# Where h and the tiles after it begin in on-chip memory, and when the first projection weights are made ready

## The chip, the cores and the metric

The kernel runs on one core of a Trainium2 chip. The metric is the device time of the whole program in microseconds (us), the median of several executions. The core has five engines that run side by side and wait for each other through semaphores: TensorE (PE, matrix products, with its own weight load, PEld), VectorE (DVE), ScalarE (ACT), GpSimd (POOL) and SyncE (SP, which issues nearly all of the DMAs here). Each engine takes its instructions in a fixed order that is written when the program is built.

A matrix product has a *stationary* operand, which is loaded into the array first, and a *moving* operand, which streams past it. Both are read from the on-chip memory (128 partitions; an address here is a byte offset within a partition).

## The reference

One layer of a hybrid decoder over 1024 tokens of width 1024, all in float32:

```
h = RMSNorm(x)
z = h @ W_in                       # 1024 -> 8224 columns
A = rwkv7(z_a)                     # time mixing, 8 heads x 64, delta-rule state
B = rglru(z_bx) * gelu(z_by)       # conv of width 4, then a linear recurrence
C = dilated_attention(z_q,z_k,z_v) # three head groups, joined by softmax sums
x = x + W_out(sum_b sigmoid(z_g[b]) * P_b(y_b))     # P_b: proj_a, proj_b, proj_c
x = x + W_down(relu(W_up RMSNorm(x))^2)             # 1024 -> 4096 -> 1024
```

## The kernel before, in words

Every large product is made of three products in a faster 32-bit format: an operand is split into a high and a low part (`A.copy(hi, raw)` on ACT, then `raw - hi` on DVE or POOL), and `mm3` issues high x high, high x low and low x high into the same PSUM bank (lines 234 to 236). `load_w` (lines 220 to 228) fetches a weight block into `wraw` (two buffers), and splits it into `whi` and `wlo` (three buffers each).

The stages, with the names under which the profile shows their matmuls:

- to 52 us: RMSNorm and the transposes (`nt_m`), which write h, transposed and split, into eight tiles `hh`, `hl` (high and low; two halves of the width, two of the tokens; 8 KB a partition each).
- 52 to 174 us: branch B (`g_bx`, `g_by`); from 130 us the projections of branch A (`g_xwa`, `g_xg`, `g_k`, `g_r`, `g_v`), then its recurrence (`ac`, `rg`, `z` and others), with the attention's projections (`g_z`, `v`) as filler between its steps, to 804 us. In `v` the h tile is stationary and the weights (256 columns) move; in the other projections the weights are stationary and 512 tokens of h move.
- 804 to 1151 us: the attention, with the merge gates (`gate_z`, matmuls `zg`) as filler. `gate_z` makes its first two of twelve pairs of column blocks plainly, and the other ten by seven block products in place of eight, for which it builds the combinations `zT1` to `zT4` of h.
- 1151 to 1272 us: `gates`, the three branch projections (`pj`) in four rounds over the output columns, in each the branches B, A, C; the branch outputs `y` come from DRAM through `wraw` (`load_y`: DMA, cast on ACT, subtraction on DVE or POOL by turns) and are split into tiles that take the places of the combinations (`y1T2`, `y1T1`, `y0T3`) or lie in a pool of their own (`yp`).
- 1272 to 1365 us: `wo`, the product with `w_out`, whose stationary operand is the merged sum (`mh`, `ml`, in the places of h).
- 1365 to 1686 us: the up product (`ux`, `uy`, `uz`), also by seven block products, with moving operands `B11`, `B21`, `T2`, `T1`, `T3`, `B22`, `T4`.
- 1686 to 2006 us: the down product (`dx`, `dy`, `dz`), in which `du`, the split activations, are stationary and the weights move.

On-chip memory is given out as two stacks. The left stack grows upwards: `cp` (constants: `cg`, `par`, `der`, `sst` and a tile of padding), `wp` (the weight buffers), then the pools of the stage. The right stack grows downwards from the end: pool `hT` with the eight h tiles, and below it `hS` for the combinations. When h is no longer used, other tiles take its eight places: `zT4`, then `mh` and `ml`, and in the tail whatever has a tag `r0` to `r7`; the tail's tags `l0` to `l12` lie in the left stack. The tail's operands are

```
operand("B11", "l8", "l9")   operand("B21", "l10", "l11")
T2: ("r5", "r6")   T1: ("l1", "r4")   T3: ("l6", "l7")   B22: ("l12", "l0")   T4: ("r7", "l2")
uring = ("r5", "r6", "l1", "r4")      # the places of du, in turn
```

where the first tag is the high part and the second the low part.

In the program before, the end of the right stack is at byte 229,344 = 224 x 1024 - 32. All tiles of `hT` and `hS` have sizes that are multiples of 1 KB, so each of them begins 992 bytes into a KB. `wp` begins at 19,456 = 19 x 1024, and the matmul operands in `wp`, in `yp` and under the `l` tags all begin at multiples of 1 KB.

The order around the second part of the change: in the last of the twelve pairs of `gate_z`, after its second block product, `late[0]()` is called, which loads the four tiles of `yb`. The weights of the first projection block (`p10`, from `proj_b`) are loaded after that, as the first thing in `gates`. All of these loads, and those of `ya`, `yc` and the next weights, go through the two `wraw` buffers in the order of the program.

Of the kernel before, what the change touches and what calls it, by code (L numbers as in the profile page):

```python
# [10 lines left out]
F32 = mybir.dt.float32  # L11
# [7 lines left out]
P = 128  # L19
# [105 lines left out]
def hybrid_block(ctx, tc, io, out, dbg=None):  # L125
# [4 lines left out]
    cp = ctx.enter_context(tc.tile_pool(name="cp", bufs=1))  # L130
    wp = ctx.enter_context(tc.tile_pool(name="wp", bufs=1))
    dr = ctx.enter_context(tc.tile_pool(name="dr", bufs=1, space=DRAM))
    pg = ctx.enter_context(tc.tile_pool(name="pg", bufs=2, space=PSUM))
# [6 lines left out]
    yb_d = dr.tile([LW, T], F32, name="yb_d")  # L140
    yc_d = dr.tile([2 * P, T], F32, name="yc_d")
# [7 lines left out]
    io = dict(io)  # L149
    io["st_d"] = dr.tile([3, 2, 32, P], F32, name="st_d")  # L150
    th_d = dr.tile([3, KT, P, T], F32, name="th_d")

    hpool = tc.tile_pool(name="hT", bufs=1, side="right")
    hp = hpool.__enter__()

# [18 lines left out]

    par = cp.tile([P, N_PAR], F32, name="par")
    der = cp.tile([P, 64], F32, name="der")

    sst = cp.tile([P, 3, 2, 2, 2, 8], F32, name="sst")

    cp.tile([P, 120], F32, name="pad")  # L180
    V.memset(der[:, 63:64], 1.0)
    A.activation(der[:, 63:64], der[:, 63:64], AF.Sqrt)
    rows = lambda ap: ap.rearrange("o (r c) -> (o r) c", c=P)
# [55 lines left out]
    def load_cols(w2d, c0, n, nm, E=G):  # L239
        return load_w(w2d[:, c0 : c0 + n].rearrange("(k p) c -> p k c", p=P), [P, KT, n], nm, E)  # L240
# [42 lines left out]
    with tc.issue_after(done.ins):  # L283
        w0 = {(0, x): load_cols(w_in, c, P, f"w0{x}", V) for x, c in enumerate((C_BX, C_BY))}
# [39 lines left out]
    gt = gt_p.__enter__()  # L324
    h2_p = tc.tile_pool(name="hS", bufs=1, side="right")
    h2 = h2_p.__enter__()
    late = []
# [3 lines left out]
    yp = yp_p.__enter__()  # L331
    ys = {}

    def load_y(src, b, ks, place):

        for k in ks:
            r = wp.tile([P, T], F32, tag="wraw", name=f"yr{b}{k}", bufs=2)
            S.dma_start(r, src[k * P : (k + 1) * P, :])
            h, l = (place(k, x) for x in "hl")
            A.copy(h, r)  # L340
            (G if k % 2 else V).tensor_tensor(l, r, h, ALU.subtract)
            ys[(b, k)] = h, l
# [3 lines left out]
    def in_block(nm, b):  # L346

        def place(k, x):
            if k % 2 == 0:
                blocks[(b, k // 2, x)] = h2.tile([P, 2, T], F32R, tag=f"{nm[k // 2]}{x}", name=f"y{b}{nm[k // 2]}{x}")  # L350
            return blocks[(b, k // 2, x)][:, k % 2, :]
        return place

    in_yp = lambda b: lambda k, x: yp.tile([P, T], F32R, name=f"y{b}{k}{x}")
    late.append(lambda: load_y(yb_d, 1, range(4), in_block(("T2", "T1"), 1)))
    for _ in fill:
        pass

# [4 lines left out]
    mhi, mlo = ([[mt[(x, hf, k // 4)][:, k % 4, :] for hf in range(2)] for k in range(KT)] for x in range(2))  # L363
    def load_ya():
        load_y(ya_d, 0, range(2), in_block(("T3",), 0))
        load_y(ya_d, 0, range(2, 4), in_yp(0))

    last = gates(tc, io, psum, pg, gt, yp, wp, th_d, ys, mhi, mlo, load_w, mm3, {0: load_ya, 2: lambda: load_y(yc_d, 2, range(2), in_yp(2))})
    yp_p.__exit__(None, None, None)
    gt_p.__exit__(None, None, None)  # L370
    h2_p.__exit__(None, None, None)
# [969 lines left out]
            yield  # L1341


def gates(tc, io, psum, pg, gt, tp, wp, th_d, ys, mhi, mlo, load_w, mm3, loads):

    nc = tc.nc
    V, A, G, S = nc.vector, nc.scalar, nc.gpsimd, nc.sync
    names = {1: "proj_b", 2: "proj_c", 0: "proj_a"}
    turn = 0
    for p in range(KT // 2):  # L1350
        sums = {}
        for b in (1, 0, 2):
            kn = 2 if b == 2 else 4
            w = io[names[b]][0][:, 2 * p * P : (2 * p + 2) * P]
            wh, wl = load_w(w.rearrange("(k p) c -> p k c", p=P), [P, kn, 256], f"p{b}{p}")
            if p == 0 and b in loads:
                loads[b]()
            tiles = [(m, hf) for m in (2 * p, 2 * p + 1) for hf in range(2)]
            bk = [pg.tile([P, 512], F32, tag="g", name=f"pj{b}{p}{i}") if i < 2 else psum("w", 2, f"pj{b}{p}{i}") for i in range(4)] if turn % 2 else [
                psum("s", 2, f"pj{b}{p}{i}") if i < 2 else psum(f"ac{i - 2}", 1, f"pj{b}{p}{i}") for i in range(4)]  # L1360
            turn += 1
            for (m, hf), ps in zip(tiles, bk):
                sl, ms = slice(hf * H, hf * H + H), slice(m % 2 * P, (m % 2 + 1) * P)
                th = (tp.tile([P, H], F32, tag="tb", name=f"tb{b}{m}{hf}", bufs=8) if b == 1 else
                      gt.tile([P, H], F32, tag="th", name=f"tg{b}{m}{hf}", bufs=5))
                last = S.dma_start(th, th_d[b, m, :, sl])
                mm3(ps, [(wh[:, k, ms], wl[:, k, ms], ys[(b, k)][0][:, sl], ys[(b, k)][1][:, sl]) for k in range(kn)])
                V.scalar_tensor_tensor(th, th, 1.0, ps, ALU.add, ALU.mult)
                if b == 1:
                    sums[(m, hf)] = th  # L1370
                    continue
                s = sums[(m, hf)]
                V.tensor_tensor(s, s, th, ALU.add)
                if b == 2:
                    A.activation(mhi[m][hf], s, AF.Copy, scale=0.5)
                    V.scalar_tensor_tensor(mlo[m][hf], s, 0.5, mhi[m][hf], ALU.mult, ALU.subtract)
    return last
# [378 lines left out]
```

## Time and profile before

| | us |
|---|---|
| median of three runs (lowest, highest) | 1999.5 (1998.18, 2002.98) |
| the profiled execution | 2007.88 |
| its span, first to last instruction | 2006.1 |
| PE busy | 1937.7 |
| DVE busy | 1240.2 |
| POOL, ACT busy | 773.7, 762.8 |
| granted TensorE clock, mean share | 0.985 |

The profile is of one execution. A row of a group of instructions reads: line, engine, operation, output <- inputs by the program's names, shape, count, then busy us, mean ns of one instruction, idle time of the engine just before them and what ended it. A row in order of time reads: start us, duration us, engine, line and so on. Matmuls are pipelined: the drawn duration of one reaches into the next ones, so the pace of a run of them is read from the distance of their starts. In the windows' rows, each engine's busy time is followed by the number of instructions.

### The profile page before, as it was taken

The numbers are of one execution on the slowest core, as the hardware profiler recorded it, in microseconds if no ns is written. First come the engines' busy times: TensorE is split into PE (matmuls) and PEld (weight loads), VectorE is DVE, ScalarE is ACT, GpSimd is POOL, SyncE is SP. The second block draws the span as 40 slices with busy tenths as digits, with TensorE's granted clock in tenths as the row PEclk, the third lists the DMA queues.
The fourth block names the chain that finished last, engine by engine and source line by source line (L and its number), as shares of the span: only waits on it lengthen the run. The fifth ranks groups of instructions, "written<-read, shape, count | busy, mean of one in ns | idle before, by whom it ended". The sixth has DMA issues, their size and how long they took to land. (4 is left out here: it accounts for less than half of the span.)

```text
span 2006.1 us, 29767 instructions
## 1 busy us (share of the span) xinstructions
PE 1937.7 (97%) x11634; PEld 1515.7 (76%) x11634; DVE 1240.2 (62%) x1992; ACT 762.8 (38%) x1275; POOL 773.7 (39%) x631
## 2 busy tenths in 40 slices
PE   8999999999999999999999899999999999999999
PEld 6776777786677778777767668887788888788887
DVE  5555446556566554775454456347876677987875
ACT  5675323233323322445454321245233233333332
POOL 1343533443343340622532442344334344544542
PEclk9999999999999998999999999999999999999999
DMA  4122312221221221434442664542444439535231
GB/s 145 53 70 70 102 37 61 63 62 51 51 59 50 65 54 42 129 105 149 143 134 90 190 225 158 184 158 105 158 168 147 147 144 366 194 125 188 85 126 63
DMA packets 191618, 236.53 MB, mean 118 GB/s; under 512 B 38536, under 2 KB 133413, under 8 KB 191478
## 3 DMA queue, kind: packets, MB, share of 16 engines
q1 hardware_dynamic: 191302, 234.62, 35.6%
q8 instruction: 91, 1.49, 0.3%
q14 instruction: 49, 0.40, 0.1%
q0 software_dynamic: 160, 0.02, 0.0%
q10 hardware_dynamic: 16, 0.00, 0.0%
HBM read 168.14 MB, written 68.82 MB: 118 GB/s over the span
## 5 line engine op out<-in xcount | busy, mean ns | idle before, releaser
L1476 POOL TENSOR_TENSOR wl_d<-dr,wh_d 128x1024 fp32r<-128x1024 f32 x40 | 102.4, 2560 | 131.7 <-ACT wh_d L1475 131.7
L1285 POOL TENSOR_TENSOR wz<-wr_z,wz 128x512 fp32r<-128x512 f32 x60 | 82.5, 1375 | 169.3 <-ACT wz L1284 145.5
L1476 DVE TENSOR_TENSOR du<-dq,du 128x1024 fp32r<-128x1024 f32 x56 | 123.7, 2208 | 26.9 <-ACT du L1475 26.9
L234 PE MATMUL dx<-wh_d,du 128*128 128x512 f32 x256 | 101.6, 397 | 2.6 <-DVE acc L1656 2.6
L235 PE MATMUL dx<-wl_d,du 128*128 128x512 f32 x256 | 101.2, 395 | 0.0
L236 PE MATMUL dx<-wh_d,du 128*128 128x512 f32 x256 | 101.1, 395 | 0.0
L1475 ACT CAST wh_d<-dr 128x1024 fp32r<-128x1024 f32 x40 | 42.0, 1050 | 145.3 <-PE dx L236 75.5
L771 DVE TENSOR_SCALAR s<-ac,wc 64x64 f32<-64x64 f32 x128 | 36.0, 281 | 71.8 <-PE ac L767 69.4
L235 PE MATMUL g_z<-hl,wh_z 128*128 128x512 f32 x192 | 77.9, 406 | 0.0
L236 PE MATMUL g_z<-hh,wl_z 128*128 128x512 f32 x192 | 77.7, 405 | 0.0
L234 PE MATMUL g_z<-hh,wh_z 128*128 128x512 f32 x192 | 77.2, 402 | 0.4 <-DVE zsq L426 0.4
L1476 POOL TENSOR_TENSOR wl_a<-ur,wh_a 128x1024 fp32r<-128x1024 f32 x15 | 47.3, 3156 | 72.9 <-ACT wh_a L1475 72.9
L1476 POOL TENSOR_TENSOR wl_s<-ur,wh_s 128x1024 fp32r<-128x1024 f32 x16 | 41.7, 2608 | 82.1 <-ACT wh_s L1475 82.1
L227 POOL TENSOR_TENSOR wl_wo<-wr_wo,wh_wo 128x1024 fp32r<-128x1024 f32 x16 | 39.2, 2452 | 64.6 <-ACT wh_wo L226 64.5
L1475 ACT CAST du<-dq 128x1024 fp32r<-128x1024 f32 x56 | 58.6, 1046 | 3.3 <-DMA dq<-u_d 3.3
L1656 DVE TENSOR_TENSOR acc<-dx,acc 128x512 f32<-128x512 f32 x64 | 42.0, 679 | 28.3 <-PE dx L236 28.3
L234 PEld LDWEIGHTS dx<-wh_d,du 128*128 128x128 f32 x256 | 48.4, 189 | 14.3 <-DVE acc L1656 3.0
L234 PE MATMUL v<-wh_wv,hh 128*128 128x256 f32 x192 | 56.3, 293 | 1.3 <-DVE st L777 1.3
L235 PEld LDWEIGHTS dx<-wl_d,du 128*128 128x128 f32 x256 | 48.4, 189 | 11.4
L236 PEld LDWEIGHTS dx<-wh_d,du 128*128 128x128 f32 x256 | 48.3, 189 | 11.5
L1022 DVE SCALAR_TENSOR_TENSOR lg<-l,sst,bias 128x128 f32<-128x128 f32 (+1 forms) x96 | 34.3, 403 | 36.2 <-PE pt L1042 27.5
L235 PE MATMUL v<-wl_wv,hh 128*128 128x256 f32 x192 | 55.6, 290 | 0.0
(757 smaller groups left out, 6213.6 us busy)
## 6 DMA issues: line engine op xcount, KB each, us to landing
dq<-u_d SPq DMA_DIRECT2D x56, 512.0 KB
wr_z<-in_w_in_dram SPq DMA_DIRECT2D x32, 512.0 KB
ur<-in_mlp_up_dram SPq DMA_DIRECT2D x16, 1024.0 KB
dr<-in_mlp_down_dram SPq DMA_DIRECT2D x16, 1024.0 KB
th_d<-th SPq DMA_DIRECT2D x48, 256.0 KB
tg<-th_d SPq DMA_DIRECT2D x32, 256.0 KB
wr_wo<-in_w_out_dram SPq DMA_DIRECT2D x16, 512.0 KB
qk_d<-zo SPq DMA_DIRECT2D x24, 256.0 KB
```

What stands on the lines that cost most here:

```text
L227: E.tensor_tensor(lo, raw, hi, ALU.subtract)
L234: PE.matmul(ps, lh, rh, start=first and i == 0, stop=False, skip_group_check=skip)
L235: PE.matmul(ps, lh, rl, start=False, stop=False, skip_group_check=skip)
L236: end = PE.matmul(ps, ll, rh, start=False, stop=last and i == n - 1, skip_group_check=skip)
L771: V.tensor_scalar(ns[half[h], :], pb[h][half[h], 128 * j + 64 * c : 128 * j + 64 * c + 64], wc[half[h], 2 * i + c : 2 * i + c + 1], None, ...
L1022: V.scalar_tensor_tensor(lg[:, q, lo:256], pls[h][:, 256 * q + lo : 256 * q + 256], rqk[:, 8 * h + s : 8 * h + s + 1], bias[:, h, lo:256], ...
L1285: (V if i == 2 else G).tensor_tensor(l, src, h, ALU.subtract)
L1475: A.copy(hi, src)
L1476: split.last = E.tensor_tensor(lo, src, hi, ALU.subtract)
L1656: V.tensor_tensor(acc[row][:, half[col]], ps, acc[row][:, half[col]], ALU.add)
```

## The change

It has two parts. The tile `sst` (768 bytes a partition), until now in `cp`, and a padding tile of 224 bytes are put into a new pool at the end of the right stack, ahead of `hT`; the padding in `cp` shrinks from 480 to 224 bytes. So the right stack begins 992 bytes lower and `hT`, `hS` and all that takes their places begin at multiples of 1 KB; `cp` is 1024 bytes shorter, and the left stack begins a whole KB lower. And the weights `p10` are loaded and split in `late[0]()`, ahead of the four `yb` loads, and handed to `gates` as `w0`.

```diff
+    cr = ctx.enter_context(tc.tile_pool(name="cr", bufs=1, side="right"))
+
+    sst = cr.tile([P, 3, 2, 2, 2, 8], F32, name="sst")
+    cr.tile([P, 56], F32, name="padr")
     hpool = tc.tile_pool(name="hT", bufs=1, side="right")
     hp = hpool.__enter__()
...
     der = cp.tile([P, 64], F32, name="der")
-
-    sst = cp.tile([P, 3, 2, 2, 2, 8], F32, name="sst")
-
-    cp.tile([P, 120], F32, name="pad")
+    cp.tile([P, 56], F32, name="pad")
...
-    late.append(lambda: load_y(yb_d, 1, range(4), in_block(("T2", "T1"), 1)))
+    def load_first():
+        late.append(load_w(io["proj_b"][0][:, 0:256].rearrange("(k p) c -> p k c", p=P), [P, 4, 256], "p10"))
+        load_y(yb_d, 1, range(4), in_block(("T2", "T1"), 1))
+
+    late.append(load_first)
...
-    last = gates(tc, io, psum, pg, gt, yp, wp, th_d, ys, mhi, mlo, load_w, mm3, {0: load_ya, 2: lambda: load_y(yc_d, 2, range(2), in_yp(2))})
+    last = gates(tc, io, psum, pg, gt, yp, wp, th_d, ys, mhi, mlo, load_w, mm3, late[1], {0: load_ya, 2: lambda: load_y(yc_d, 2, range(2), in_yp(2))})
...
-            wh, wl = load_w(w.rearrange("(k p) c -> p k c", p=P), [P, kn, 256], f"p{b}{p}")
+            wh, wl = w0 if (b, p) == (1, 0) else load_w(w.rearrange("(k p) c -> p k c", p=P), [P, kn, 256], f"p{b}{p}")
```

More of the change, by code (lines that the diff above doesn't have):

```diff
@@ L1341, in gate_z, with gates @@
             yield
-def gates(tc, io, psum, pg, gt, tp, wp, th_d, ys, mhi, mlo, load_w, mm3, loads):
+def gates(tc, io, psum, pg, gt, tp, wp, th_d, ys, mhi, mlo, load_w, mm3, w0, loads):
     nc = tc.nc
```

## The prediction

> **What bounds the kernel now.** I read the page's head first, then the windows by stage, then the waits of TensorE, then the matmul groups of one stage, and at last the order of time at two places.
>
> ```profile
> span 2006.1 us, 29767 instructions
> PE 1937.7 (97%) x11634; PEld 1515.7 (76%) x11634; DVE 1240.2 (62%) x1992; ACT 762.8 (38%) x1275; POOL 773.7 (39%) x631
> ```
>
> TensorE is busy in 97% of the span, and the next engine, DVE, in 62%. The span less PE's busy time leaves 2006.1 - 1937.7 = 68.4 us in which PE stands still. Where these lie, the windows say (the first engine column is PE, then PEld, DVE, ACT, POOL, the granted clock, DMA):
>
> ```profile
> 52.00:131.00 79.00, 74.62 (x312) 58.93 (x311) 42.40 (x63) 51.01 (x56) 30.11 (x15) 0.98 0.21 58
> 822.00:1104.00 282.00, 277.13 (x1412) 201.36 (x1413) 162.33 (x348) 143.43 (x398) 112.99 (x89) 0.99 0.38 119
> 1104.00:1152.00 48.00, 39.10 (x163) 30.50 (x160) 23.11 (x34) 17.75 (x29) 22.32 (x14) 0.96 0.60 187
> 1425.00:1686.00 261.00, 259.99 (x1131) 211.81 (x1130) 177.32 (x139) 82.00 (x106) 102.71 (x34) 1.00 0.49 181
> 1686.00:2006.00 320.00, 313.68 (x1347) 253.12 (x1345) 253.09 (x201) 106.60 (x107) 140.84 (x54) 0.99 0.40 144
> ```
>
> Every long stage is PE's; only the hand-over around 1104 to 1152 us is not (39.1 of 48). The page draws matmuls overlapped, so a busy PE may still be paced by something. So the question is what paces a matmul that waits for nothing.
>
> **What alignment is worth: the up stage shows it in one kernel.** By the layout of the program before, the right-hand stack ends 32 bytes below a multiple of 1 KB, so every tile there (`r0` to `r7` in the tail, all of h, its combinations, y in their places) begins 992 bytes into a KB; all matmul operands of the left stack (`wp`, the `l` tags) begin at multiples of 1 KB. In the up product the weights are stationary in `wp` and the moving operand is T2 (both halves right), T1 (h left, l right), T4 (h right, l left), T3, B22, B11, B21 (left). Same shape, same weights' place, same 260 us, with PE waiting 1 us in it:
>
> ```profile
> L234 PE MATMUL ux<-T2h,wh_s 128*128 128x512 f32 x56 | 22.3, 398 | 1.0 <-ACT c L1493 1.0
> L235 PE MATMUL ux<-T2l,wh_s 128*128 128x512 f32 x56 | 22.2, 396 | 0.0
> L236 PE MATMUL ux<-T2h,wl_s 128*128 128x512 f32 x56 | 22.1, 396 | 0.0
> ...
> L235 PE MATMUL ux<-T3l,wh_s 128*128 128x512 f32 x56 | 21.9, 391 | 0.0
> ...
> L234 PE MATMUL uz<-B22h,wh_s 128*128 128x512 f32 x56 | 21.8, 389 | 0.0
> L235 PE MATMUL uz<-B22l,wh_s 128*128 128x512 f32 x56 | 21.8, 389 | 0.0
> ...
> L236 PE MATMUL ux<-T4h,wl_a 128*128 128x512 f32 x55 | 21.8, 395 | 0.0
> ...
> L235 PE MATMUL ux<-B11l,wh_a 128*128 128x512 f32 x48 | 18.8, 391 | 0.0
> ```
>
> Off the KB a matmul takes 395 to 398 ns, on it 389 to 391: a gap of 4 to 9 ns. Since drawn durations overlap, the spacing counts:
>
> ```profile
> 1429.74 0.40 PE L234 MATMUL ux<-T2h,wh_s 128*128 128x512 f32 x1
> ...
> 1432.54 0.39 PE L234 MATMUL uz<-T1h,wh_s 128*128 128x512 f32 x1
> ...
> 1443.65 0.39 PE L234 MATMUL uz<-B22h,wh_s 128*128 128x512 f32 x1
> ...
> 1448.86 0.39 PE L236 MATMUL uz<-B22h,wl_s 128*128 128x512 f32 x1
> ```
>
> Twelve starts of T2 in 1432.54 - 1429.74 = 2.80 us are 233.3 ns each; 23 steps of B22 in 5.21 us are 226.5. So 6.8 ns, or 2.9%, per matmul of 512 columns. A stationary operand off the KB with the moving one on it shows the slow figure too (`wo`, where `mh` is stationary on the right):
>
> ```profile
> L235 PE MATMUL wo<-wl_wo,mh 128*128 128x512 f32 x128 | 50.7, 396 | 0.0
> L236 PE MATMUL wo<-wh_wo,ml 128*128 128x512 f32 x128 | 50.5, 395 | 0.0
> ```
>
> **The change, part by part.**
> *Layout.* `sst` (768 bytes a partition) and 224 bytes of padding now lie at the right end, 992 bytes in all, so the right stack begins on a KB; `cp` loses 768 + 256 = 1024 bytes, so the left stack moves by one whole KB and keeps its places. No instruction is added; `sst` is read as before. What moves to the aligned pace, counted from the loops and these rows (PE count by window; first the matmuls that read `hh`, then `hl`):
>
> ```profile
> 0.00:52.00 52.00, 24.75 (x70) 0.93 0.44 140
> 52.00:174.00 122.00, 92.86 (x284) 0.97 0.21 61
> 174.00:804.00 630.00, 333.41 (x1152) 0.98 0.22 59
> 804.00:1104.00 300.00, 112.89 (x328) 0.99 0.40 125
> 1104.00:1152.00 48.00, 13.33 (x40) 0.96 0.60 187
> ```
> ```profile
> 52.00:174.00 122.00, 57.54 (x143) 0.97 0.21 61
> 174.00:804.00 630.00, 210.87 (x576) 0.98 0.22 59
> ```
>
> `hl` has half of `hh`'s count, in each stage: 1.5 x 1874 = 2811, by the loops 2808 (a window's edge counts twice). Of them 576 are the 256-column products of `v` (24 tiles x 8 x 3), where h is stationary; 2232 have 512 columns. Further by the loops: combinations in `gate_z` 4 x 10 pairs x 12 = 480; y in their places 6 x 48 = 288; `wo` 384; up: T2 192, `T1l` 64, `T4h` 128; down: 1344, whose stationary `du` goes round `r5, r6, l1, r4`, so three in four, 1008. Sum: 2232 + 480 + 288 + 384 + 384 + 1008 = 4776 matmuls of 512.
>
> Price: the groups bound it at 4 and 9 ns, the two runs in order of time give 6.8; I take 6.0, because the `T3l` and `B11l` groups on the KB sit at 391 and not at 389. That is 4776 x 6.0 = 28.7 us. For the 576 of 256 columns no row has an aligned partner (they stand at 287 to 293 ns); bounds 0 (if the loss goes with the length read at a stretch) and 6 (one fixed loss a matmul); I take 3, 1.7 us. Sum 30.4 us if PE were alone.
>
> How much reaches the end? Where others pace, a shorter matmul only lengthens PE's wait. To 174 us (532 matmuls of h; norm, DVE and ACT chains), in 1104 to 1182 us (60 + 96 of `gate_z`, 72 of y) and in the opening of up (48) I count half: 808 x 6.0 / 2 = 2.4 us lost. In the stretches where a recurrence or softmax is interleaved (174 to 1104 us: 1152 + 492 + 384 = 2028 matmuls and the 576), PE is nearly always busy (277 of 282 us in the softmax's stretch) and the others mostly wait for it, as the scan's step shows: DVE waited 69 us for PE there, PE 2.2 for DVE.
>
> ```profile
> L771 DVE TENSOR_SCALAR s<-ac,wc 64x64 f32<-64x64 f32 x128 | 36.0, 281 | 71.8 <-PE ac L767 69.4
> ```
> ```profile
> PE ac L764 <- DVE s L771: 2.2, 4, 0.8
> ```
>
> There I take off 15% of 13.9 us, 2.1 us. The other 1940 (rest of y, `wo`, up, down: 11.6 us) pass in full; DVE covers down with 253 of 320 us. Kept: 30.4 - 2.4 - 2.1 = 25.9 us. What the places do to DVE, ACT, POOL and the DMAs I cost at nothing: none of them is the bound of a long stage, so a few per cent of theirs, up or down, vanish in their slack (in down DVE has 320 - 253 = 67 us).
>
> *The first projection weights in the last pair.* `load_w` of `proj_b` (one 512 KB DMA on SP, one 1.05 us cast on ACT, one 2.4 us subtraction on POOL) moves from behind the four `yb` loads to ahead of them, past SP, ACT and POOL queues; nothing is added.
>
> ```profile
> 1131.12 0.40 PE L236 MATMUL zg<-zT2h,wz 128*128 128x512 f32 x1
> 1133.12 1.26 POOL L1285 TENSOR_TENSOR wz<-wr_z,wz 128x512 fp32r<-128x512 f32 x1
> 1135.92 0.79 PE L234 MATMUL zg<-zT1h,wz 128*128 128x512 f32 x1 [4.40 <-DVE th L1328]
> 1136.60 3.52 POOL L1121 TENSOR_TENSOR yc<-yc,yt 128x512 f32<-128x512 f32 x2 [2.22 <-DVE yc L1116]
> 1145.52 0.41 SPq L223 DMA_DIRECT2D wr_p<-in_proj_b_dram  x1
> 1150.69 1.04 ACT L226 CAST wh_p<-wr_p 128x1024 fp32r<-128x1024 f32 x1 [1.26 <-DMA wr_p<-in_proj_b_dram]
> 1151.79 0.50 PE L234 MATMUL pj<-y1T2h,wh_p 128*128 128x512 f32 x1 [3.05 <-ACT wh_p L226]
> 1152.59 0.63 PE L235 MATMUL pj<-y1T2l,wh_p 128*128 128x512 f32 x1
> ...
> 1156.00 0.39 PE L236 MATMUL pj<-y1T2h,wl_p 128*128 128x512 f32 x1
> 1175.77 1.56 SPq L338 DMA_DIRECT2D yr<-yc_d  x2
> ```
>
> PE waits 3.05 us for these weights and then runs eight matmuls in 1156.00 - 1152.59 = 3.41 us, 0.43 us each (drawn 0.63 long) and not 0.23: 1.6 us more. 4.6 us is the upper bound. (The clock gate of the Trainium skill, "TensorE: Matmul & The Clock Gate", "What's actually happening", halves the clock after an idle window of about 3.4 us; the rows after both waits agree.) But the raw weights and y go through two `wraw` buffers, each load waiting for the POOL or DVE subtraction two loads back, down to the `yc` loads at 1175.77, and putting the weights first leaves as many loads in this chain. If POOL makes their low half only behind `yc` (1136.60 + 3.52 = 1140.1, done at 1142.5), the second `yb` load is late next, and some 2 us may be lost: lower bound -2. PE's first 36 matmuls cover the late fourth `yb` tile; then y of A is waited for instead. I take +2.
>
> Sum: 25.9 + 2 = 27.9 us. The profiled execution is 2007.9 us (span 2006.1 and 1.8 around it) and would be 1980.0; it stands 8.4 above the median of the runs, 1999.5, from which the same 27.9 leaves 1971.6.
>
> **The rivals.**
> *A: the layout changes nothing.* Then the slow pace belongs to the right stack's high addresses, not to the 32 bytes, and only the weights count: 1999.5 - 2 = 1997.5. For it: no right-hand tile is seen aligned. Against it: `B22h` lies above 150 KB in the partition, between the places where `zT1` was slow, and is fast. The Trainium skill speaks for it twice: by "TensorE: Matmul & The Clock Gate" ("Wait — 56ns, not 53.3ns?") a warm matmul starts every N / 2.4 GHz + 2.5 ns, 215.8 ns for 512, wherever its operands lie; by "SBUF — State Buffer" ("Specifications (TRN2)") lines have 16 bytes, and 992 is a multiple of that. The trace agrees with neither: 226.5 and 233.3 ns stand side by side.
> *B: the pace falls, but the gain stops at others' waits.* PE's 68.4 us of standing then grow: half of 30.4 lost, none from the weights, 1999.5 - 15.2 = 1984.3. For it: 2028 of the matmuls are filler between chains of others. Against: the scan's waits above.
> *C: slower.* With weights and h beginning at the same offset in the KB, weight load and moving read would meet at the same place and each matmul would lose the 6.8 ns once more: 4776 x 6.8 = 32.5 us, 2032. It decides as soon as pairs on the KB are slower than mixed ones. Against: `B22` with `wp` is such a pair, and the fastest.
>
> **How the numbers follow.** Forecast 0.73, B 0.13, A 0.09, C 0.05. The range: 4 ns in place of 6 gives 1999.5 - 17 - 2 = 1980; with 6.8 for all, 3.5 for the narrow ones, nothing lost and 4.6 for the weights, 32.5 + 2.0 + 4.6 = 39 and 1960.5. The likeliest case alone is 1961 to 1981; with B 1961 to 1988, leaving out A and C (0.14). About 0.3% (6 us) is what a measurement here can tell: forecast and B are faster by more; A splits into 0.07 same, 0.01 faster, 0.01 slower; C is slower. Faster 0.87, same 0.07, slower 0.06.
>
> **What the changed profile would show.** Right: `T2`, `T4` and `wo` groups at 389 to 391 ns like `B22`; `g_z` (402 to 406 now) lower by about 6; the down stage some 6 us shorter than 320, up 2 to 3; no wait of `pj` for `wh_p` at its start, but one for a y tile within 20 us. Wrong: these groups at 395 and more (A), or all at 400 (C); or the groups fall and the waits of PE grow by 10 us and more (B).

## The result, and the profile after

| | before | changed |
|---|---|---|
| median (lowest, highest), four runs each, us | 2001.24 (1998.18, 2005.46) | 1982.83 (1979.91, 1986.43) |
| ratio, with its 95% interval | | 0.9907 (0.988 to 0.9935) |
| profiled execution, us | 2007.88 | 1979.91 |
| its span, us | 2006.1 | 1978.1 |

The changed kernel is faster by 0.93%, some 18.6 us (13 to 24 by the interval). The forecast was 1971.6, with a range from 1961 to 1988. The sign holds. The time lies inside the range only because the range took in rival *B*; the likeliest case alone was 1961 to 1981, and 1982.83 is outside it. A third of the forecast gain of 27.9 us is missing. (The forecast was taken from a median of 1999.5 over three runs; with the fourth the kernel before stands at 2001.24, which is 1.7 of the 11.2 us between forecast and result.) In the ratios below one execution is left out, of the kernel with the right stack 64 bytes off: it took 3733.11 us, its nine others 1995.61 to 2002.65.

The two profiled spans differ by 28.0 us, which looks like the forecast exactly, but it isn't: the profiled execution of before lies above all four of its runs in the table, that of the changed kernel is the quickest of its four (granted clock 0.985 and 0.988; the other three took 1980.97 at 0.987, 1984.69 and 1986.43 at 0.985). A difference of two spans holds that spread, so the reading below goes by the pace of the matmuls (the time from the start of one to the start of the next) and not by the spans.

The head of the page after:

```profile
span 1978.1 us, 29765 instructions
PE 1906.3 (96%) x11634; PEld 1512.1 (76%) x11634; DVE 1237.5 (63%) x1992; ACT 763.5 (39%) x1275; POOL 774.5 (39%) x631
```

As many matmuls as before, 31.4 us less of TensorE's drawn time, and 1978.1 - 1906.3 = 71.8 us of standing still, 3.4 more than before. The windows of the softmax's stretch, the up stage and the down stage (320 us long before, 310 now):

```profile
822.00:1104.00 282.00, 275.74 (x1436) 202.84 (x1435) 162.46 (x356) 146.84 (x406) 117.39 (x91) 1.00 0.38 120
1425.00:1686.00 261.00, 261.00 (x1154) 216.10 (x1153) 183.77 (x142) 83.30 (x106) 106.05 (x35) 1.00 0.51 194
1668.00:1978.00 310.00, 305.84 (x1349) 252.58 (x1347) 248.06 (x199) 106.75 (x107) 138.97 (x54) 1.00 0.40 147
```

In the same 282 us lie 1436 matmuls for 1412, in the same 261 us 1154 for 1131, and the down stage needs 310 us for what took 320. (The windows are fixed in time and the stages begin earlier now: the last 17 us of the second window belong to the down product already.) The groups of matmuls in the up stage, where the moving operands T2, T1 and T4 stood beside T3, B22 and B11 at another figure:

```profile
L238 PE MATMUL ux<-T4h,wl_a 128*128 128x512 f32 x58 | 22.6, 389 | 0.0
L236 PE MATMUL ux<-T2h,wh_s 128*128 128x512 f32 x56 | 21.9, 391 | 0.6 <-ACT c L1499 0.6
...
L237 PE MATMUL ux<-T3l,wh_s 128*128 128x512 f32 x56 | 21.8, 389 | 0.0
L236 PE MATMUL uz<-B22h,wh_s 128*128 128x512 f32 x56 | 21.8, 389 | 0.0
```

All are alike now. In the groups of the whole program, the drawn means of `g_z` and `v` (filler between the steps of other chains) have changed little, that of `wo` by 6 ns:

```profile
L237 PE MATMUL g_z<-hl,wh_z 128*128 128x512 f32 x192 | 77.4, 403 | 0.0
...
L237 PE MATMUL v<-wl_wv,hh 128*128 128x256 f32 x192 | 55.6, 290 | 0.0
...
L237 PE MATMUL wo<-wl_wo,mh 128*128 128x512 f32 x128 | 49.9, 390 | 0.0
```

In the trace of before, the same `g_z` and `v` groups:

```profile
L235 PE MATMUL g_z<-hl,wh_z 128*128 128x512 f32 x192 | 77.9, 406 | 0.0
...
L235 PE MATMUL v<-wl_wv,hh 128*128 128x256 f32 x192 | 55.6, 290 | 0.0
```

So three things had to be explained: whether the layout is all of the gain, what it is in the layout that counts, and why the filler gains so little.

**The measure used below.** Drawn durations overlap, so for every split-format matmul (the ones that `mm3` issues, and the 48 of `zss` in the attention's projections) the distance from its start to the next start was taken, cut off at 245 ns (128 ns for 256 columns) where something else came between, and added up by stage. The rest of the span is waits, other matmuls and cut-off ends. This sum is called the pace sum below. In us:

| stage | before | layout only (below) | difference |
|---|---|---|---|
| start to the first `g_k` | 134.6 | 132.8 | 1.8 |
| from there to the last `v` | 350.0 | 347.1 | 2.9 |
| to the last `zg` | 242.5 | 238.5 | 4.0 |
| `pj` | 111.7 | 109.7 | 2.0 |
| `wo` | 89.6 | 87.2 | 2.4 |
| up | 309.2 | 305.4 | 3.8 |
| down | 311.4 | 304.5 | 6.9 |
| all | 1549.0 | 1525.2 | 23.8 |

The pace sum is a steady figure: it is 1525.0 in the changed kernel and 1524.9 in a second profile of it, and 1549.1 in the kernel with the weights alone, while the rest of the span moves between 451 and 461 us from one execution to the next.

### The profile page after: what moved, and what is told of

The parts are those of the page before. It is cut to its first block, busy times and chain, and to the rows that moved or that the text cites. A ratio compares the mean times of both kernels' runs of the same rounds, so it can differ in the third digit from the quotient of the medians.

```text
span 1978.1 us, 29765 instructions
## 1 busy us (share of the span) xinstructions
PE 1906.3 (96%) x11634; PEld 1512.1 (76%) x11634; DVE 1237.5 (63%) x1992; ACT 763.5 (39%) x1275; POOL 774.5 (39%) x631
## 4 chain that ended last, share of the span: by engine, by line
PE 77%; DVE 8%; DMA 6%; ACT 3%; issue 3%; POOL 3%; SPq 1%; DVEq 0%; ACTq 0%; POOLq 0%
PE dx L236 3%; PE dx L237 3%; PE dx L238 3%; PE zg L236 3%; PE ux L236 3%; PE ux L237 3%; PE ux L238 3%; PE zg L237 3%; PE zg L238 3%; PE g_z L237 2%; PE g_z L236 2%; PE g_z L238 2%; PE wo L238 1%; PE wo L236 1%; PE dz L237 1%
## 5 line engine op out<-in xcount | busy, mean ns | idle before, releaser
L238 PE MATMUL v<-wh_wv,hl 128*128 128x256 f32 x192 | 55.3, 288 | 0.0
```

Source lines behind the costliest of these rows:

```text
L238: end = PE.matmul(ps, ll, rh, start=False, stop=last and i == n - 1, skip_group_check=skip)
```

## The experiments

The first theory was the prediction's: a matmul is quick if its operands begin at multiples of 1 KB, whatever the other operand does. Its rival: only the difference between the starts of the stationary and the moving operand counts. In the two kernels on hand both say the same, since the left stack begins on a KB and the right one either with it or 32 bytes below. (Strictly only the tiles of the left stack begin on a KB. A stationary block of 128 columns is 512 bytes wide, so every second one in `wp` begins 512 bytes into a KB, and `B22`, which uses both kinds, was quick in the kernel before. So the first theory, taken at its word, already didn't fit.) For the size of the gain there was a third question: whether a quick pair is quick from its first matmul on, or only in a long run.

The first four kernels ran on one chip (before: 2005.32 us there), the next two on another (before: 2003.73); the last three leave the whole layer out and only time matmuls.

### The two halves of the change, and the change again

Layout alone, from the kernel before:

```diff
+    cr = ctx.enter_context(tc.tile_pool(name="cr", bufs=1, side="right"))
+    sst = cr.tile([P, 3, 2, 2, 2, 8], F32, name="sst")
+    cr.tile([P, 56], F32, name="padr")
...
-    sst = cp.tile([P, 3, 2, 2, 2, 8], F32, name="sst")
-    cp.tile([P, 120], F32, name="pad")
+    cp.tile([P, 56], F32, name="pad")
```

> The layout part alone: h and what takes its places at multiples of 1 KB, the first projection weights loaded where they were. Theory 1 (the layout carries the whole gain; the weights' part is eaten by the chain of loads through the two wraw buffers): 18 to 22 us under the kernel before, the same as the whole change within 2 us; T2, T4 and wo groups at 389 to 391 ns; PE's wait of about 3 us for wh_p is back, and no wait of 4 us for y0T3h. Theory 2 (the weights carry the 4.6 us that the wait and the slow clock behind it cost): 13 to 15 us under, 4 to 5 us behind the whole change.

Weights alone: the changed kernel with the lines above undone.

> The weights' part alone: layout as before, proj_b's first weights loaded and split in the last pair. Theory 1: within 1 us of the kernel before; the wait for wh_p goes and waits for y1T1l and y0T3h of together 4 to 6 us stand in its place. Theory 2: 4 to 5 us faster. Groups T2, T4, wo stay at 395 to 398 ns under both. It is also a second profile of the old layout: the down stage (first dx to the end) took 315.5 us in the profile before and 305.2 after; if 6 to 7 us of these 10 are pace and the rest is one wait of that execution, this profile shows 312 to 316.

The changed kernel once more, beside them:

> The whole change once more, beside the others on one chip: 18 to 22 us under the kernel before. In the two profiles the spans differ by 28.0 us; if 6 to 8 of these are the clock that each execution happened to be granted (0.985 before, 0.988 after), the timed difference stays near 20; if the change itself raised the clock, it comes near 28.

| kernel | median, us | ratio to before (95%) |
|---|---|---|
| layout only | 1984.26 | 0.9898 (0.9883 to 0.9912) |
| weights only | 2006.58 | 1.0005 (0.9996 to 1.0014) |
| changed, again | 1984.5 | 0.9892 (0.9873 to 0.9911) |

The layout is the whole gain; the weights bring nothing that the interval can tell. The order in time of the changed kernel at the place where they were moved shows why:

```profile
1125.40 0.79 PE L236 MATMUL zg<-zT1h,wz 128*128 128x512 f32 x1 [4.90 <-DVE th L1334]
...
1148.32 0.50 PE L237 MATMUL pj<-y1T1l,wh_p 128*128 128x512 f32 x1 [1.26 <-POOL y1T1l L343]
...
1154.97 1.55 PE L236 MATMUL pj<-y0T3h,wh_p 128*128 128x512 f32 x4 [4.55 <-ACT y0T3h L342]
...
1170.31 1.19 PE L236 MATMUL pj<-y20h,wh_p 128*128 128x512 f32 x4 [2.44 <-ACT y20h L342]
```

and the end of the same stretch before the change:

```profile
1180.45 2.08 PE L234 MATMUL pj<-y20h,wh_p 128*128 128x512 f32 x4 [2.55 <-ACT y20h L340]
```

The wait of 3.05 us for `wh_p` is gone, and two stand in its place, for `y1T1l` (1.26) and `y0T3h` (4.55). From the restart of `zT1h` to the first `y20h` it is 1170.31 - 1125.40 = 44.91 us, and before 1180.45 - 1135.92 = 44.53. Behind the second wait the matmuls start 0.43 us apart again (at 1156.82, 1157.25 and 1157.68), as they did behind the wait of before. The number of loads through the two raw buffers hasn't changed, and the last of them is ready no sooner. The waits of TensorE in the kernel with the weights alone and in that with the layout alone (us in total, times, longest) show the two forms of the same thing:

```profile
PE pj L233 <- ACT y0T3h L339: 5.6, 1, 5.6
...
PE pj L233 <- ACT wh_p L225: 0.5, 1, 0.5
```
```profile
PE pj L235 <- ACT wh_p L227: 4.9, 3, 3.7
```

### The right stack 64 bytes off

From the changed kernel, 16 words less padding: h and all in its places begin 64 bytes into a KB, the left stack stays on it.

```diff
-    cr.tile([P, 56], F32, name="padr")
+    cr.tile([P, 40], F32, name="padr")
```

> The changed kernel with the right-hand padding cut by 64 bytes: h and what takes its places begin 64 bytes into a KB, no longer at multiples of 1 KB; the left stack stays at multiples of 1 KB. Theory 1a (a start at a multiple of 64 bytes is all that is needed): time as the whole change within 2 us, T2, T4, wo groups at 389 to 391 ns. Theory 1b (the whole KB, or 128 bytes and more, is needed): groups back at 394 to 398 ns and the time 15 to 20 us slower than the whole change. The v products (256 columns, h stationary) stand 117.2 ns apart in the profile before and 119.6 after: if two operands at the same offset in the KB cost them the 2.4 ns, they return to 117 here.

2000.03 us, ratio 0.9967 (0.9957 to 0.9977): most of the gain is lost, with `sst` still on the right and the weights still early. The groups of the up stage, and `wo` and `v` of the whole program:

```profile
L236 PE MATMUL ux<-T2h,wh_s 128*128 128x512 f32 x56 | 22.2, 396 | 0.5 <-ACT c L1499 0.5
...
L237 PE MATMUL ux<-T2l,wh_s 128*128 128x512 f32 x56 | 21.8, 390 | 0.0
...
L236 PE MATMUL uz<-B22h,wh_s 128*128 128x512 f32 x56 | 21.8, 389 | 0.0
...
L237 PE MATMUL ux<-T4l,wh_a 128*128 128x512 f32 x54 | 21.4, 397 | 0.0
```
```profile
L237 PE MATMUL wo<-wl_wo,mh 128*128 128x512 f32 x128 | 50.7, 396 | 0.0
...
L237 PE MATMUL v<-wl_wv,hh 128*128 128x256 f32 x192 | 54.9, 286 | 0.0
```

`wo`, which reads one operand from each stack, is back at 396, and `B22h`, with both on the left, stays at 389. The drawn means of T2 lie between (390 to 396). By the starts, T2 takes 229.5 ns here, 233.4 before and 227.2 in the changed kernel, while `wo` is back at 233.3, as before. So a moving operand 64 bytes ahead of the stationary one (T2, the projections of h and the gates) loses less than a stationary one 64 ahead of the moving one (`wo`, three quarters of down). The pace sum, some 1539, lies between 1549.0 and 1525.0, and what is left of the gain lies in the stages where h or T2 moves. `T4l` with `wh_a` lies wholly on the left and is slow all the same, in this kernel and in before (394): it stands between two products of `T4h`, so a slow pair seems to cost its neighbour too (more on this under the last experiment). This run shows that the offset is the cause. Both theories expected it, so it doesn't tell them apart.

### Everything 992 bytes into a KB

From the kernel before, 32 bytes less padding in `cp`: now the left stack too begins 992 bytes into a KB, and no matmul operand of the large products lies on one.

```diff
-    cp.tile([P, 120], F32, name="pad")
+    cp.tile([P, 112], F32, name="pad")
```

> The kernel before with 32 bytes less padding at the end of cp: now the left stack's matmul operands begin 992 bytes into a KB too, like h. Nothing begins at a multiple of 1 KB any more, but the two operands of a matmul begin at the same place in their KB again. Theory A (each operand must itself begin at a multiple of the KB): all groups of the up stage, T3 and B22 included, at 394 to 398 ns, and the time 3 to 8 us over the kernel before. Theory R (only the difference of the two starts counts): all groups at 389 to 391 ns and the time 17 to 23 us under the kernel before, as with the layout part alone.

1988.74 us, ratio 0.9919 (0.9904 to 0.9934), and in the up stage:

```profile
L235 PE MATMUL ux<-T2l,wh_s 128*128 128x512 f32 x49 | 19.1, 389 | 0.0
L236 PE MATMUL ux<-T4h,wl_a 128*128 128x512 f32 x48 | 18.7, 389 | 0.0
L235 PE MATMUL uz<-B22l,wh_s 128*128 128x512 f32 x48 | 18.7, 389 | 0.0
```

With that the theory by multiples of 1 KB fell: nothing lies on one, and these groups stand at 389. The pace sum is 1525.6 us, that of the new places. So one constant in a padding tile does to the pace all that the layout part of the change did. In time it brought 15.0 us (16 by the ratio), just under the 17 to 23 that were expected; the interval overlaps that of the layout alone (0.9883 to 0.9912), and the few us that may be missing lie in the rest of the span (461 us), not in the pace.

### The right stack 768 bytes off

From the changed kernel: h at 768 bytes into a KB, the left stack on it (and a padding of the tail shortened by as much, so that all fits).

```diff
-    cr.tile([P, 56], F32, name="padr")
+    cr.tile([P, 120], F32, name="padr")
...
-    sm.tile([P, 168], F32, name="pad1")
+    sm.tile([P, 104], F32, name="pad1")
```

> The changed kernel with 256 bytes more padding at the right end (and as many fewer in the tail's small pool): h and what takes its places begin 768 bytes into a KB, the left stack at multiples of 1 KB. If starts that differ by a quarter of a KB are as good as equal ones (the places count in steps of 256 bytes or fewer, and 64 bytes was too little), the time is that of the whole change within 2 us and wo stands at 389 to 390 ns; if the whole or half KB counts, wo stands at 394 to 398 and the time is 5 to 20 us over the whole change.

1986.08 us, ratio 0.9916 (0.9902 to 0.993), the pace sum 1525.4, and `wo`, whose operands now lie 768 bytes apart:

```profile
L237 PE MATMUL wo<-wl_wo,mh 128*128 128x512 f32 x128 | 50.0, 390 | 0.0
```

By the pace 768 costs nothing, and 32 and 64 do. The period is shorter than 1 KB. The time was to be that of the whole change within 2 us; by the ratios it is some 5 us longer (0.9916 on this chip, 0.9892 on the other, the intervals overlap), with the same pace sum.

### Pairs of offsets by themselves

One large tile on a KB, in which 36 matmuls in a row take a stationary operand at offset S and a moving one at offset M; each pair twice, the second time in reversed order.

```
so = s // 4 + 256 * (k // 2 % 8)
mo = 4096 + m // 4 + 1024 * (k % 4)
PE.matmul(ps[:, 0:n], big[:, so : so + P], big[:, mo : mo + n], ...)
```

> The disputed cost by itself: all of the layer's work is left out; one tile of split numbers that begins at a multiple of 1 KB, and series of 36 matmuls (stationary 128 x 128, moving 512 columns in wide, 256 in half), in which the stationary operand begins S and the moving one M bytes into a KB, each series twice and the second time in reverse order. Names: a 0, b 32, c 64, d 96, e 128, f 256, g 384, h 512, i 768, j 992. Theory A: wide series with S or M off a multiple (b, j) stand at 395 to 398 ns, Sb_Mb and Sj_Mj too; Theory R: Sb_Mb, Sc_Mc, Sj_Mj at 389 like Sa_Ma, and Sc_Mb, Se_Mc slow. Under both Sj_Ma and Sa_Mj are slow (395 and more), Sh_Ma is fast. Half series: Sa_Ma some 2 to 5 ns slower than Sc_Ma, as v was (119.6 against 114.9 ns from start to start).

The order in time has one row for a series, so the pace is the distance of two rows over 36. The letters after S and M are the offsets in bytes: a 0, b 32, c 64, d 96, e 128, f 256, g 384, h 512, i 768, j 992.

```profile
33.37 8.55 PE L149 MATMUL wide_Sb_Ma_x<-big 128*128 128x512 f32 x36
41.76 8.56 PE L149 MATMUL wide_Sc_Ma_x<-big 128*128 128x512 f32 x36
...
66.96 8.38 PE L149 MATMUL wide_Sf_Ma_x<-big 128*128 128x512 f32 x36
75.17 8.53 PE L149 MATMUL wide_Sg_Ma_x<-big 128*128 128x512 f32 x36
83.54 8.32 PE L149 MATMUL wide_Sh_Ma_x<-big 128*128 128x512 f32 x36
91.70 8.33 PE L149 MATMUL wide_Si_Ma_x<-big 128*128 128x512 f32 x36
...
380.82 8.35 PE L149 MATMUL wide_Sb_Mb_y<-big 128*128 128x512 f32 x36
389.02 8.56 PE L149 MATMUL wide_Sa_Mj_y<-big 128*128 128x512 f32 x36
397.42 0.85 PE L149 MATMUL wide_Sa_Mi_y<-big 128*128 128x512 f32 x3
```

32 bytes apart (Sb with Ma) it is (41.76 - 33.37) / 36 = 233 ns a matmul; both at 32 (Sb with Mb) (389.02 - 380.82) / 36 = 228; 256 apart (75.17 - 66.96) / 36 = 228; 384 apart (83.54 - 75.17) / 36 = 232.5; 512 apart 226.7; 992 apart (397.42 - 389.02) / 36 = 233. Without the first six of a series, every pair whose starts differ by a multiple of 256 bytes takes 226.6 to 227.4 ns (b, c, h and j with themselves, and f, h, i with a), and of the others all take 232 to 235 but one: the moving operand 64 ahead of the stationary one takes 228.9, in both rounds. (The stationary one 64 ahead takes 233.3. This is the split that the kernel with the right stack 64 bytes off had shown.) So the difference counts, modulo 256 bytes. The two prices that the up stage of before had shown, 226.5 and 233.3, are here with nothing else running.

For 256 columns the picture is another: with equal places 119.8 to 120.0 ns, with others 116.6 to 118.8, but for two: with the moving operand 96 ahead 120.0, and with it 64 ahead 117.8 in one round and 113.3 in the other. There equal places cost more than most others.

### The difference in finer steps

The same with the stationary operand at 0 and the moving one in steps of 16 bytes and a few others.

> The disputed cost by itself, finer: all of the layer's work is left out; series of 36 matmuls with the stationary operand at a multiple of 1 KB and the moving one M bytes past one, each series twice, the second time in reverse order (wide: 512 columns, a stationary operand used twice; each: 512 columns, a new one each time; half: 256 columns). M by letter: a to p are 0 to 240 in steps of 16; q 4, r 8, s 24, t 40, u 56, v 72, w 200. From the first series: 226.7 ns from start to start at differences that are multiples of 256 bytes, 228.8 at 64, 232 to 234 at 32, 96, 128. Theory R1 (equal places modulo 256 bytes are the best there is): no M below 226 in wide and each. Theory R2 (some distance lets the weight load slip past the moving read altogether): an M with 216 to 222. Half: 113 to 120, the 113.3 that M = 64 showed in one of its two series either comes back in both or belongs to how the series began.

Letters: a 0, b 16, e 64, f 80, p 240, q 4, r 8.

```profile
32.85 8.50 PE L149 MATMUL wide_Mb_x<-big 128*128 128x512 f32 x36
41.19 8.57 PE L149 MATMUL wide_Mc_x<-big 128*128 128x512 f32 x36
...
57.99 8.42 PE L149 MATMUL wide_Me_x<-big 128*128 128x512 f32 x36
66.24 8.47 PE L149 MATMUL wide_Mf_x<-big 128*128 128x512 f32 x36
...
150.09 8.33 PE L149 MATMUL wide_Mp_x<-big 128*128 128x512 f32 x36
158.26 8.68 PE L149 MATMUL wide_Mq_x<-big 128*128 128x512 f32 x36
166.78 8.57 PE L149 MATMUL wide_Mr_x<-big 128*128 128x512 f32 x36
```

16 bytes: (41.19 - 32.85) / 36 = 232 ns; 64: 229; 4: (166.78 - 158.26) / 36 = 237, the slowest in both rounds; 240: 227 here, and 236.8 in the second round, the only offset that changed sides. The others between 8 and 224 took 229.9 to 235.6. Nothing is quicker than 226.7, so for 512 columns a difference of 0 modulo 256 is the best of those tried. A new stationary operand for each matmul, in place of one used twice, gives the same figures, the two of 240 bytes included (226.7 and 236.8); 48 bytes took 233.4 in the first round and 230.0 in the second, in both kinds of series. The order of the series was reversed in the second round, so what runs before may decide; no run here settles it.

For 256 columns 192 bytes give 113.3 in both rounds, against 120 for 0. But the difference alone doesn't fix these: the same difference modulo 256 (the stationary operand 64 ahead) took 117.8 in both rounds of the first series, and 64 took 117.8 here. The slowest is 4 bytes (122.8), and 24, 40, 56 and 80 stand at 120 too. In the kernel with the right stack 64 bytes off, `v` has this difference of 192 and takes 114.9.

### How long a quick pair takes to become quick

Six times in a row, eight plain float32 matmuls of 128 columns, and then 2, 4, 8, 16 or 32 split-format ones, at a difference of 0 or of 32.

```
for k in range(8):
    PE.matmul(tiny[:, 0:P], raw[:, 0:P], raw[:, P : 2 * P], ...)
for k in range(ns):
    PE.matmul(ps, big[:, so : so + P], big[:, mo : mo + 512], ...)
```

> What a switch costs, by itself: all of the layer's work is left out; blocks of 2, 4, 8, 16 or 32 split matmuls of 512 columns behind eight plain float32 matmuls of 128 columns each, six blocks a series, each series twice; both operands at multiples of 1 KB (Ma) or the moving one 32 bytes past (Mb). Theory S (after a switch the pace of equal places has to settle: 231 to 236 ns for the first matmuls, 226.7 only after 8 to 10): Ma is no faster than Mb in blocks of 2 and 4 (within 1 ns from start to start), 2 to 3 ns faster in blocks of 8, 4 in blocks of 16, 5 in blocks of 32. Rival (the interleaved stages lose their gain to other engines' reading of the same memory, not to the switches): Ma is 6 to 7 ns faster in every block length, since here no other engine works.

In order of time, two blocks of four and two of 32 (Ma: difference 0, Mb: 32); the time of a block is the distance from its row to the next `tiny`:

```profile
49.17 1.17 PE L155 MATMUL four_Ma_x<-big 128*128 128x512 f32 x4
50.18 1.95 PE L151 MATMUL tiny<-raw 128*128 128x128 f32 x16
...
65.46 1.17 PE L155 MATMUL four_Mb_x<-big 128*128 128x512 f32 x4
66.47 1.95 PE L151 MATMUL tiny<-raw 128*128 128x128 f32 x16
...
488.57 7.71 PE L155 MATMUL thirtytwo_Mb_y<-big 128*128 128x512 f32 x32
496.12 1.95 PE L151 MATMUL tiny<-raw 128*128 128x128 f32 x16
...
543.72 7.53 PE L155 MATMUL thirtytwo_Ma_y<-big 128*128 128x512 f32 x32
551.09 1.95 PE L151 MATMUL tiny<-raw 128*128 128x128 f32 x16
```

Four take 1.01 us either way. Thirty-two take 551.09 - 543.72 = 7.37 against 496.12 - 488.57 = 7.55 us, 5.6 ns each. In the means over all blocks, eight gain 2.3 ns each (1929 against 1947 ns a block) and sixteen 4.5 (3742 against 3814). Blocks of two take 543 to 552 against 545 to 558 ns, on average some 2.5 ns less for each matmul, where no gain was expected. By place in the block, the first takes 314 to 316 ns in either kind, then the pair at 0 takes 236, 228, 232, 231 and from the sixth on 227; the pair at 32 stays at 231 to 235. So the quick pace comes only after some five matmuls without a switch. This is called settling below.

The other format isn't needed for it. In the series of offsets, where no plain matmul stands between, most of the quick pairs also begin with matmuls of 223 to 237 ns before they stand at 227: ten of them with both operands at 64 in the second round, none with the stationary operand at 768. What sets that number isn't shown. That a pair can need several matmuls to become quick fits `T4l`, which stands between two products of `T4h`.

The changed kernel shows the same between 180 and 1100 us, where some 240 runs of split matmuls stand between the chains' small ones: the second and third after a switch take 232 to 233 ns on average, the fifth to seventh 229, and from the eleventh on 227. Before, it was 232 to 233.6 at every place. The late places reach 227 there with all engines at work, so it isn't the other engines' reading of the memory that keeps the filler slow.

## Why the prediction was right, and what of it was off

**The bound.** It holds: the layout changes TensorE's pace, and the time follows. TensorE stands still for 71.8 us after 68.4.

**The price and the count (28.7 for 512 columns).** This is the term that was mis-sized. Counted, with `v`, were 30.4 us if TensorE were alone; the pace sum fell by 24.0 (1549.0 to 1525.0). By stage, in the order of the table, the forecast at 6.0 ns was 3.2, 8.6 (1.7 of it for `v`), 6.2, 1.7, 2.3, 2.3, 6.0; measured stands in the table's last column. Where the products run long, `pj` to down, 15.1 us came for 12.3: there the price is nearer the 6.8 ns of the two runs (down: 6.9 us / 1008 = 6.8), and up gains more than was counted because all of its T1 and T4 products had been slow, not only those whose moving part lay on the right: 576 matmuls with T2, not 384. In the first three stages 8.7 us came for 18.0: `v` is 3.1 of the missing 9.3, and the products of 512 columns brought 10.1 for 16.3. The prediction had taken 226.5 ns from a run of 24 matmuls and 233.3 from one of 12, in the up stage, and priced the filler with it. But the filler comes in short runs. Of its 2760 matmuls of 512 columns 2314 are followed by another one, and these went from 232.9 to 228.8 ns: settling keeps them 4.9 us above the 226.7 of a long run. Behind the other 446 comes something else or a wait, and there the starts show no gain. The prediction had foreseen a loss in these stages (15% for others' chains), but not this one. That the two errors, too little for the long runs and too much for the filler, partly cancel is luck.

**The 256-column products (1.7 us gained).** The sign was wrong. `v` goes from 117.2 to 119.6 ns from start to start, 576 x 2.4 = 1.4 us lost, and with 64 bytes of difference it was 114.9. Its drawn means (290 before and after) don't show it. The lower bound of 0 should have gone below nothing, as no row had excluded a loss.

**What the end sees (4.5 us lost of the gain).** Of the 23.8 us of pace, the layout alone brings 20.5 to the end by the ratio (17.7 to 23.5). The missing 3.3 is little more than the interval leaves open, and which wait holds it, if any, isn't settled: the waits named in the traces change by as much from one execution to the next. The down stage is an instance. It became 10 us shorter and not 6, and the pace is 6.9 of it. Most of the other 3 is a wait, 26 us into the stage, that this profile of before has and this profile of after hardly has (2.6 us against 0.4; behind it seven matmuls take 3.09 us, from 1712.78 to 1715.87, in place of 1.6). It is seen in this row of before and its answer after:

```profile
L234 PE MATMUL dx<-wh_d,du 128*128 128x512 f32 x256 | 101.6, 397 | 2.6 <-DVE acc L1656 2.6
```
```profile
L236 PE MATMUL dx<-wh_d,du 128*128 128x512 f32 x256 | 99.7, 389 | 0.4 <-DVE acc L1662 0.4
```

The pace doesn't set this wait: the kernel with h at 768 bytes has the new pace and waits 3.6 us at that place, the one with h at 64 bytes has the old pace in this stage and waits 0.2. The kernel with the weights alone, the second profile of the old layout, waits 3.1. What sets it stays open.

**The weights (+2 us).** They were worth nothing (-2.8 to +0.8 us by the interval), within the bounds of -2 and 4.6. The reason against it stood in the text: two buffers, and as many loads in the chain. The y tile that it said would come late came late, and took back the whole gain and not a part. The +2 was a choice between the bounds without a row for it.

**The rivals.** *A*, no effect of the layout, is out. But its reason for doubt was sound: the prediction called the cause "on the KB", and the kernel with everything at 992 bytes shows that as the wrong name. The count was right only because the left stack happened to lie on a KB. The two rules of the Trainium skill that it cited stay apart from the trace: "TensorE: Matmul & The Clock Gate" ("Wait — 56ns, not 53.3ns?") gives 215.8 ns for 512 columns and has no term for where the operands begin, and the quickest here is 226.7. The lines of 16 bytes of "SBUF — State Buffer" ("Specifications (TRN2)") don't give the step that counts either: 16 bytes of difference cost 5 ns here. *B*, the gain lost in others' waits, isn't shown: the median, 1982.83, is near its 1984.3, but TensorE's standing grew by 3.4 us and not by 15. The filler of 512 columns did lose some 6 of its 16 us, but in the pace itself and not in waits of others. *C*, equal places collide, is false for 512 columns, where equal places are the quickest, and true in small for the 256 of `v` (2.4 ns each).

**The signs.** T2, T4 and `wo` went to 389 to 391 and down and up got shorter, as said (up by 3.8 in pace). `g_z` was to fall by about 6 and its `hl` group fell by 3 in the drawn mean (406 to 403), by 4.1 in the starts (232.9 to 228.8): the one sign that came out otherwise, and the one that led to the settling. The wait of `pj` went from the weights to the y tiles: `pj` begins at 1132.34 us and waits for them up to 1148.32 and 1154.97, 16 and 23 us in, the longer one a little later than the 20 us that were said.

## What to carry to other kernels

Before a kernel whose large products are bound by TensorE is restaged, look at where its stationary and its moving operands begin: for 512-column products in this format the starts should differ by a multiple of 256 bytes, and one padding tile of the right size (here 32 bytes less) is worth 3% of each matmul in a long run. For 256 columns equal places cost more than most others and no single difference was always the best, so time the pair in question. Price such a gain by the length of the runs: blocks of four between other matmuls gained nothing, of eight a third of the 6.6 ns of a long run, and of 32 over four fifths. And read a change of pace from the starts: the drawn means hid that of `v` and showed too little of that of `g_z`.

## What the runs showed of the hardware that was not expected

- The pace of a split-format matmul of 512 columns depends on the difference of its operands' starts modulo 256 bytes: 226.7 ns at 0, 228.9 with the moving one 64 ahead, 230 to 237 at most others, worst at 4 bytes. The sides need not be on any round address.
- With 256 columns equal places cost more than most others: 120 ns at 0, 122.8 at 4 bytes, and between 113.3 and 117.8 at 192, so the difference alone doesn't fix it there.
- After plain float32 matmuls the first split-format one takes 314 to 316 ns, and the quick pace comes only from about the sixth on. Without plain ones between, a series of quick pairs needed none to ten matmuls to settle.
- At 240 bytes the same series took 227 ns in one round and 236.8 in the other. What decides between the two states is open, as is the mechanism behind the 256 bytes: the runs show where the time goes, and not what in the memory or the array takes it.
